# RWKV time mixing on one Trainium2 core: where a unit's columns lie in the mixed tiles of four batches

## The chip, the core and the metric

The kernel runs on one core of a Trainium2 chip. The metric is the device time of one execution in microseconds (us). The five engines of the core are written as in the profile: PE is TensorE (matmuls; PEld is its loading of weights), DVE is VectorE, ACT is ScalarE, POOL is GpSimd, SP is the queue that only starts transfers here. Each engine works through its own list of instructions in order, and the engines wait for each other by semaphores, which are counters that an instruction raises when it is done.

## The reference

Every token is mixed with the token before it, in two mixtures that matter here (the key projection never reaches the output):

```python
xv = x * time_mix_v + x_prev * (1 - time_mix_v)
xr = x * time_mix_r + x_prev * (1 - time_mix_r)
v = xv @ value_weight
r = xr @ receptance_weight
out = (sigmoid(r) * v) @ output_weight
```

x has 16 batches of 2048 tokens with 256 features. Features are the contraction of the first two products, so the tokens are transposed first: features on the 128 partitions, in two halves called `ko` 0 and 1, tokens along the columns.

## The kernel before

**Units and pairs.** The work is cut into 64 units of 512 tokens (`TU`), four to a batch; two units make a pair. Three tiles matter for each pair. `xt` holds the transposed tokens. `mix` holds the two mixtures m = 0 (receptance) and m = 1 (value) of a pair: 128 partitions, and per m and `ko` 1024 columns, so m takes 2048 elements of a partition's row, with `ko` 0 in the first 1024 of them and `ko` 1 in the second. `mix` rotates over three buffers. `z_sb` holds sigmoid(r) * v of one unit.

**A mixture is a product and a sum.** The token mix is folded into the weights: the tile needs only (previous token) * c plus (token). The product, one per pair, m and `ko`, covers 1024 columns and goes to DVE (`scale`, L353), ACT (`scale_act`, L631) or POOL (`scale_pool`, L363). The sum (`add`, L375) is one DVE instruction per unit and m, over both `ko`, 1024 elements, in place on `mix`.

**One unit on PE.** In program order, for unit g: four matmuls of 512 columns into `psum_r` (`project`, L383, m = 0; the order is output half, then `ko` 0, `ko` 1), eight matmuls of 256 columns into `psum_o` for unit g - 2 (`out_matmuls`, L412), four matmuls into `psum_v` (L383, m = 1). `psum_r`, `psum_v` and `psum_o` have one buffer each. ACT takes the sigmoid of `psum_r` (L651) and copies `psum_o` out (L464); DVE makes `z_sb` from the sigmoid and `psum_v` (L690).

**One unit on DVE.** From unit 10 on, the order in iteration g is: at even g the product of m = 0, `ko` 0 for the pair that begins with g + 2; then the sum of m = 1 for unit g + 1 (in the code `sums`); then `z_sb` of unit g; then the sum of m = 0 for unit g + 2 (in the code `held`). POOL makes one product in each iteration, after the sum of m = 1, and ACT one product at even g.

**The batches concerned.** Batches 10 to 13 (`STAGED_PAIRS`), units 40 to 55, eight pairs, get their transposed tokens by DMA from a copy in DRAM, as plain columns in the order of the tokens. Their stores want each partition to hold runs of tokens, so unit h of a pair takes columns q * 8 + h * 4 + i (q from 0 to 127, i from 0 to 3): runs of four columns, one run in two. `tokens` gives the view of `xt`, `mixed` the view of `mix`, and both use `unit_cols`. Products over a pair take all 1024 columns; sums and matmuls of one unit take its runs. Batches 14 and 15 and all earlier ones keep runs of 128 columns.

**Order.** The program order is written out by hand and not changed by a scheduler; the waits are derived from it by the framework, which looks at which columns of a tile each instruction reads and writes.

Of the kernel before, what the change touches and what calls it, by code (L numbers as in the profile page):

```python
# [15 lines left out]
def kernel(  # L16
# [31 lines left out]
    UJ = 4  # L48
    TU = UJ * P
# [63 lines left out]
    xt = {}  # L113
# [199 lines left out]
    def slots(piece, off=0):  # L313

        b, _, lo, hi = piece
        j = lo // P + (lo // TU if b < BYUNIT else 0) + off
        return slice(j, j + (hi - lo) // P)

    def unit_cols(cols, lo, hi):

        if hi - lo > TU:
            return cols
        assert hi - lo == TU
        return cols.rearrange("p k (q h i) -> p k q h i", h=2, i=UJ)[:, :, :, lo // TU % 2]

    def tokens(piece, off, ko=None):

        b, _, lo, hi = piece
        if b in STAGED_PAIRS:
            pair = lo // (2 * TU) * 2 * TU + off  # L330
            cols = unit_cols(xt[b][:, :, pair : pair + 2 * TU], lo, hi)
            return cols if ko is None else cols[:, ko]
        if b < STAGED:
            cols = xt[b][:, slots(piece, off)]
        else:
            cols = xt[b][:, :, off + lo : off + hi].rearrange("p k (j c) -> p j k c", c=P)
        return cols if ko is None else cols[:, :, ko]

    def mixed(piece, ko=None):
        b, m, lo, hi = piece  # L340
        cols = mix[(b * S + lo) // (2 * TU)][:, m]
        if b in STAGED_PAIRS:
            cols = cols.rearrange("p j k c -> p (j k c)").rearrange("p (k t) -> p k t", k=KO)
            cols = unit_cols(cols, lo, hi)
            return cols if ko is None else cols[:, ko]
        j = lo // P % (2 * UJ)
        cols = cols[:, j : j + (hi - lo) // P]
        return cols if ko is None else cols[:, :, ko]

    def scale(piece, kos=(0, 1)):  # L350
        b, m, _, _ = piece
        for ko in kos:
            nc.vector.tensor_scalar(  # L353
                out=mixed(piece, ko),
                in0=tokens(piece, 0, ko),
                scalar1=c_sb[:, m, ko : ko + 1],
                scalar2=None,
                op0=ALU.mult,
            )

    def scale_pool(piece, after):
        b, m, _, _ = piece
        op = nc.gpsimd.tensor_scalar(  # L363
            out=mixed(piece, 1),
            in0=tokens(piece, 0, 1),
            scalar1=c_sb[:, m, 1:2],
            scalar2=1.0,
            op0=ALU.mult,
            op1=ALU.mult,
        )  # L370
        tc.add_manual_dep(op.ins, after.ins.name, SYNC, reason="one at a time")

    def add(piece):
        b = piece[0]
        return nc.vector.tensor_tensor(  # L375
            out=mixed(piece), in0=mixed(piece), in1=tokens(piece, 1), op=ALU.add
        )
# [261 lines left out]
    for g in range(NU - 1):  # L639
# [61 lines left out]
        if g in STAGE_AT:  # L701
            b = STAGE_AT[g]
# [41 lines left out]
```

## Time and profile before

| what | value |
|---|---|
| median of three runs | 200.34 us (200.04 to 200.56) |
| the profiled execution | 200.75 us, span of its instructions 198.9 us |
| PE busy | 193.8 us, 97% |
| DVE busy | 183.8 us, 92% |
| ACT busy | 177.0 us, 89% |
| POOL busy | 86.8 us, 44% |
| sum, L375, on `xt_both` | 112 of 696 ns |
| product on DVE, L353, 1024 columns | 40 of 481 ns |
| product on POOL, L363, 1024 columns | 54 of 1121 ns |
| product on ACT, L631, 1024 columns | 14 of 1161 ns |

The span runs from the first instruction to the last; 1.85 us of the profiled time lie outside it. A matmul's record is longer than its turn: records of one group overlap, so the time from one group's start to the next is what the group costs on PE.

### The profile page before, as it was taken

What the parts mean: (1) busy time and instruction counts of PE and PEld (TensorE: products, weight loads), DVE (VectorE), ACT (ScalarE), POOL (GpSimd) and SP (SyncE); (2) the same over time, 40 slices, a digit from 0 to 9 for tenths busy, and PEclk for the clock granted to TensorE, in tenths of its full rate; (3) what the DMA queues carried; (4) which work ended last, traced back from release to release, by engine and by line L of the source; (5) the groups of instructions that cost most, each with busy time, mean ns of one, the idle gap of its engine ahead of it and who ended that gap; (6) DMA issues with size and microseconds to landing.
All of it is one profiled execution on the core that took longest, in us unless ns stands there. A gap on an engine that the chain in (4) does not pass through costs nothing.

```text
span 198.9 us, 3759 instructions
## 1 busy us (share of the span) xinstructions
PE 193.8 (97%) x1368; PEld 123.5 (62%) x1368; DVE 183.8 (92%) x287; ACT 177.0 (89%) x197; POOL 86.8 (44%) x117
## 2 busy tenths in 40 slices
PE   8999999999999999999999999999999999999992
PEld 4656676666666666666666566656655666666661
DVE  0899999999999999999999999999999999999972
ACT  3699899999999999999999999998888888899972
POOL 2846442443675634624424474444443344444200
PEclk9999999999999999999999999999999999999998
DMA  5999999999999999999999999999999999999585
GB/s 176 236 184 216 221 278 274 270 256 260 247 384 272 292 315 321 290 226 222 234 276 290 416 293 222 208 273 228 290 340 420 415 412 422 415 417 413 244 319 202
DMA packets 36553, 58.13 MB, mean 292 GB/s; under 512 B 26068, under 2 KB 27448, under 8 KB 32312
## 3 DMA queue, kind: packets, MB, share of 16 engines
q1 hardware_dynamic: 32368, 41.34, 59.7%
q0 software_dynamic: 4016, 16.44, 41.2%
q8 instruction: 10, 0.16, 0.3%
q10 hardware_dynamic: 152, 0.13, 0.2%
q14 instruction: 7, 0.06, 0.1%
HBM read 34.34 MB, written 39.90 MB: 373 GB/s over the span
## 4 chain that ended last, share of the span: by engine, by line
PE 87%; DVE 5%; DMA 3%; SPq 1%; issue 1%; POOL 1%; ACT 1%; DVEq 0%; POOLq 0%
PE psum_v L383 26%; PE psum_r L383 26%; PE psum_o L412 26%; PE ps_t L271 7%; DMA w_f<-in_value_weight_dram 3%; DVE z_sb L690 2%; DVE mix L375 1%; DVE mix L353 1%; SPq L173 1%; PE ps_t L412 1%; ACT s_sb L651 1%; PE ps_t L383 0%; POOL x_bf L161 0%; POOL mix L363 0%; DVE w_bf L587 0%
## 5 line engine op out<-in xcount | busy, mean ns | idle before, releaser
L363 POOL TENSOR_SCALAR mix<-xt_both,c_sb 128x1024 bf16<-128x1024 bf16 (+1 forms) x55 | 61.2, 1113 | 86.8 <-DVE mix L375 74.4
L690 DVE TENSOR_TENSOR z_sb<-s_sb,psum_v 128x1024 bf16<-128x1024 bf16 (+1 forms) x64 | 76.7, 1199 | 3.4 <-PE psum_v L383 2.5
L375 DVE TENSOR_TENSOR mix<-mix,xt_both 128x1024 bf16<-128x1024 bf16 x112 | 76.8, 696 | 1.4
L383 PEld LDWEIGHTS <-w_bf 128*128 128x128 bf16 x516 | 48.7, 97 | 40.2 <-DVE mix L375 0.8
L651 ACT ACTIVATE s_sb<-psum_r 128x1024 bf16<-128x1024 f32 x63 | 65.2, 1035 | 7.5 <-PE psum_r L383 7.2
L383 PE MATMUL psum_v<-mix,w_bf 128*128 128x512 bf16 (+1 forms) x256 | 65.9, 379 | 0.1
L383 PE MATMUL psum_r<-mix,w_bf 128*128 128x512 bf16 (+1 forms) x252 | 64.8, 379 | 0.2 <-DVE mix L375 0.2
L412 PE MATMUL psum_o<-wo_bf,z_sb 128*128 128x256 bf16 x486 | 63.3, 272 | 0.2 <-DVE z_sb L690 0.2
L412 PEld LDWEIGHTS <-z_sb 128*128 128x128 bf16 x512 | 51.7, 103 | 18.6 <-DVE z_sb L503 0.7
L464 ACT COPY o_sb<-psum_o 128x1024 f32<-128x1024 f32 x50 | 51.2, 1024 | 5.1 <-PE psum_o L412 5.1
L288 ACT COPY xt_both<-ps_t 128x1024 bf16<-128x1024 bf16 x32 | 32.8, 1036 | 0.0
L271 PEld LDWEIGHTS <-x_bf 128*128 128x128 bf16 x304 | 19.8, 98 | 8.6 <-DMA x_bf<-in_x_dram 0.7
L271 PE MATMUL ps_t<-ident,x_bf 128*128 128x128 bf16 x304 | 22.7, 219 | 0.3 <-DMA x_bf<-in_x_dram 0.3
L353 DVE TENSOR_SCALAR mix<-xt_both,c_sb 128x1024 bf16<-128x1024 bf16 (+1 forms) x47 | 21.2, 460 | 0.0
L631 ACT ACTIVATE mix<-xt_both,c_sb 128x1024 bf16<-128x1024 bf16 x14 | 16.2, 1161 | 0.0
L375 DVE TENSOR_TENSOR mix<-mix,xt_first 128x1024 bf16<-128x1024 bf16 x15 | 10.6, 714 | 0.1
L464 ACT COPY x_bf<-psum_o 128x1024 f32<-128x1024 f32 x10 | 10.2, 1015 | 0.0
L353 DVE TENSOR_SCALAR mix<-xt_first,c_sb 128x512 bf16<-128x512 bf16 x22 | 6.6, 353 | 0.2
L288 ACT COPY xt_first<-ps_t 128x1024 bf16<-128x1024 bf16 x6 | 6.1, 1024 | 0.0
L161 POOL DMA_DIRECT2D x_bf<-in_x_dram x8 | 5.2, 656 | 0.0
L550 POOL COPY xt_first<-xt_first 128x254 bf16<-128x254 bf16 x5 | 2.0, 395 | 6.8 <-DVE mix L375 6.8
L363 POOL TENSOR_SCALAR mix<-xt_first,c_sb 128x512 bf16<-128x512 bf16 x6 | 4.1, 689 | 1.5 <-DVE mix L375 1.0
(70 smaller groups left out, 54.7 us busy)
## 6 DMA issues: line engine op xcount, KB each, us to landing
out_dram<-o_sb SPq DMA_DIRECT2D x24, 1024.0 KB, 12.8
x_bf<-in_x_dram POOLq DMA_DIRECT2D x8, 1024.0 KB, 16.5
x_natural<-in_x_dram POOLq DMA_DIRECT2D x4, 1024.0 KB, 13.7
out_dram<-x_bf SPq DMA_DIRECT2D x4, 1024.0 KB, 14.5
x_natural<-in_x_dram POOLq DMA_DIRECT2D x4, 512.0 KB, 14.0
x_bf<-in_x_dram POOLq DMA_DIRECT2D x6, 256.0 KB, 6.6
out_dram<-x_bf SPq DMA_DIRECT2D x6, 256.0 KB, 2.2
o_sb<-in_x_dram SPq DMA_DIRECT2D x4, 256.0 KB, 4.1
```

Of the source, the lines that this page charges most:

```text
L161: return nc.gpsimd.dma_start(out=x_bf[b], in_=rows(b), max_dma_last_dim=run)
L271: nc.tensor.transpose(out=ps[:, jj], in_=src[:, jj, ko * P : (ko + 1) * P], identity=idn)
L288: nc.scalar.copy(out=xt[b][:, j0 : j0 + UJ], in_=ps)
L353: nc.vector.tensor_scalar(out=mixed(piece, ko), in0=tokens(piece, 0, ko), scalar1=c_sb[:, m, ko : ko + 1], scalar2=None, op0=ALU.mult,)
L363: op = nc.gpsimd.tensor_scalar(out=mixed(piece, 1), in0=tokens(piece, 0, 1), scalar1=c_sb[:, m, 1:2], scalar2=1.0, op0=ALU.mult, op1=ALU.mult,
L375: return nc.vector.tensor_tensor(out=mixed(piece), in0=mixed(piece), in1=tokens(piece, 1), op=ALU.add)
L383: nc.tensor.matmul(out=ps[:, mo, :], lhsT=w_bf[:, m, ko, mo * P : (mo + 1) * P], rhs=mixed((b, m, e * TU + lo, e * TU + hi), ko), start=(k ...
L412: nc.tensor.matmul(out=ps[:, j, :], lhsT=slot[:, ko, j], rhs=wo_bf[:, ko, :], start=(ko == 0), stop=(ko == KO - 1),)
L464: nc.scalar.copy(out=o[:, j0 : j0 + UJ, :], in_=ps)
L631: nc.scalar.activation(out=mixed(piece, ko), in_=tokens(piece, 0, ko), func=ACT.Copy, scale=c_sb[:, m, ko : ko + 1],)
L651: nc.scalar.activation(out=s_sb, in_=ps_r, func=ACT.Sigmoid)
L690: nc.vector.tensor_tensor(out=z_sb[:, :, c : c + n], in0=s_sb[:, :, c : c + n], in1=ps_v[:, :, c : c + n], op=ALU.mult,)
```

## The change

In batches 10 to 13 the two units of a pair no longer alternate in `mix` every four columns; unit 0 has columns 0 to 511 and unit 1 columns 512 to 1023. `xt` stays in token order. So a product, which covers the pair, now reads 1024 columns in one run and writes runs of four, by turns into the first and the second half; a sum reads `xt` in runs of four as before, but reads and writes `mix` in one run of 512 per `ko`; a matmul reads one run of 512. The number of instructions and their order on every engine stay as they are.

```diff
-    def unit_cols(cols, lo, hi):
+    def unit_cols(cols, order, lo, hi):
+        cols = cols.rearrange(f"p k ({order}) -> p k q h i", h=2, i=UJ)
         if hi - lo > TU:
             return cols
         assert hi - lo == TU
-        return cols.rearrange("p k (q h i) -> p k q h i", h=2, i=UJ)[:, :, :, lo // TU % 2]
+        return cols[:, :, :, lo // TU % 2]
...
-            cols = unit_cols(xt[b][:, :, pair : pair + 2 * TU], lo, hi)
+            cols = unit_cols(xt[b][:, :, pair : pair + 2 * TU], "q h i", lo, hi)
...
             cols = cols.rearrange("p j k c -> p (j k c)").rearrange("p (k t) -> p k t", k=KO)
-            cols = unit_cols(cols, lo, hi)
+            cols = unit_cols(cols, "h q i", lo, hi)
```

## The prediction

> **What bounds the kernel now.** I read the page first, then the chain of work that ended last in order of time, then the timeline of one pair. The page:
>
> ```profile
> PE 193.8 (97%) x1368; PEld 123.5 (62%) x1368; DVE 183.8 (92%) x287; ACT 177.0 (89%) x197; POOL 86.8 (44%) x117
> ...
> PE 87%; DVE 5%; DMA 3%; SPq 1%; issue 1%; POOL 1%; ACT 1%; DVEq 0%; POOLq 0%
> ```
>
> PE is busy 97% and is 87% of the chain. In the stage concerned the chain is PE alone; from it, the groups around its entry and two after its end:
>
> ```profile
> 128.29 0.86 PE psum_v L383 x4
> 129.15 0.90 PE psum_r L383 x4
> 130.05 0.87 PE psum_o L412 x8
> 130.93 0.90 PE psum_v L383 x4
> 131.83 0.90 PE psum_r L383 x4
> ...
> 172.84 0.87 PE psum_o L412 x8
> 173.71 0.86 PE psum_v L383 x4
> 174.58 0.86 PE psum_r L383 x4
> ```
>
> Units 40 to 55 begin with psum_r at 129.15. There a group of four matmuls takes 0.90 us instead of 0.86: the alternating runs of four cost PE 0.036 us a group (0.900 - 0.864). A pair takes 5.35 us here (131.83 to 137.18) and 5.20 after the stage (174.58 to 179.78). The pair around unit 46, timeline of all engines:
>
> ```profile
> 144.14 1.06 PE L383 MATMUL psum_v<-mix,w_bf 128*128 128x512 bf16 x4
> ...
> 145.05 1.06 PE L383 MATMUL psum_r<-mix,w_bf 128*128 128x512 bf16 x4
> ...
> 145.31 1.22 DVE L690 TENSOR_TENSOR z_sb<-s_sb,psum_v 128x1024 bf16<-128x1024 bf16 x1 [0.18 <-PE psum_v L383]
> ...
> 146.45 0.69 DVE L375 TENSOR_TENSOR mix<-mix,xt_both 128x1024 bf16<-128x1024 bf16 x1
> 146.53 2.13 SPq L433 DMA_DIRECT2D out_dram<-o_sb  x3
> 146.71 1.56 PEld L383 LDWEIGHTS <-w_bf 128*128 128x128 bf16 x8
> 146.82 1.06 PE L383 MATMUL psum_v<-mix,w_bf 128*128 128x512 bf16 x4
> 147.06 0.48 DVE L353 TENSOR_SCALAR mix<-xt_both,c_sb 128x1024 bf16<-128x1024 bf16 x1
> ...
> 147.45 0.69 DVE L375 TENSOR_TENSOR mix<-mix,xt_both 128x1024 bf16<-128x1024 bf16 x1
> ```
>
> psum_v of unit 45 starts at 144.14, psum_r of unit 46 follows at 145.05 without a gap. The z of unit 45 can start only when that psum_v is done (145.31); behind it on DVE comes the sum of m = 0 for unit 47 (146.45 to 147.14), then the product and the sum of m = 1 for unit 47 (147.45 to 148.14). PE needs none of these two sums before unit 47, one unit later: that distance hides DVE.
>
> [...] sums with runs of four at 146.45 take 0.69 us, as the mean of all sums, 696 ns. [...] Beside z[...] POOL runs here without stretching it (1.22 us).
>
> **The change, part by part.** *Matmuls.* 16 units x 2 groups x 0.036 us = 1.15 us less on PE.
>
> *Waits.* The compiled programs have the same instructions in the same order on all engines, and the same waits on DVE, ACT, POOL and SP. On PE they differ, in each of the eight pairs. For units 40 and 41 (counts of DVE's semaphore; 199 and 200 are unit 40's sums of m = 0 and 1, 201 is z of unit 39, 202 and 204 are unit 41's sums, 203 a product):
>
> ```
> instruction on PE                   waits for DVE, before    after
> psum_r of 40, weights of matmul 1   199                      199
> psum_r of 40, weights of matmul 2   -                        202
> psum_v of 40, matmul 1              201                      - (covered by 202)
> psum_v of 40, weights of matmul 2   -                        204
> psum_r of 41, weights of matmul 1   202                      - (covered by 202)
> ```
>
> The second matmul of an even unit reads `ko` 1 of its own half, columns 1024 to 1535. The other unit's sum writes 512 to 1023 and 1536 to 2047; the columns in between are not touched, but first to last they enclose 1024 to 1535. I infer that the framework compares these extents; the waits themselves are in the program. With alternating runs it kept the units apart. So PE waits for a sum that it doesn't need, one unit too early.
>
> *The price of the wait for 202.* Let T be the start of the last matmul of psum_v of the odd unit before: 144.14 + 3 x 0.227 = 144.82. z starts at T + 0.49, the sum of m = 0 ends at 147.14 = T + 2.32. From a DVE end to the PE start it releases is 0.05 us (the chain has issue for 0.05 us between z at 191.70 and psum_o at 191.75). So matmul 2 starts at T + 2.37. Without a wait and with contiguous reads it starts two turns after T, at T + 0.43. **The stall is 1.94 us a pair.** No cover is left: z itself needs psum_v, the last PE work before the stall, and the psum_o of the unit stands behind the waiting matmul.
>
> *The new period.* From matmul 2 to the next T: three turns (0.65), psum_o (0.87), psum_v (0.86), psum_r (0.86), psum_o (0.87), three turns (0.65) = 4.76. Period 2.37 + 4.76 = 7.13 against 5.35: +1.78. Eight pairs: **+14.2 us**; the same from the stalls less the gain, 8 x 1.94 - 1.15 = 14.4. I take 14.3.
>
> *The wait for 204.* The second sum ends 148.14 = T + 3.32, released T + 3.37. psum_v's matmul 2 is due at T + 2.37 + 0.65 + 0.87 + 0.22 = T + 4.11. It costs nothing, with 0.74 us to spare.
>
> *What is late next.* z of the even unit starts at T + 5.0 and ends at 6.25; psum_v of the odd unit needs it at T + 6.5: free. ACT: sigmoid at T + 3.2, copy of psum_o at 4.1, product at 5.0, sigmoid of the odd unit 6.1 to 7.1, needed by z at T + 7.6: 0.5 us to spare. Stores start later, none sooner. Nothing queued is recovered later, since PE is the chain on both sides of the stage.
>
> *Products.* Eight on DVE, eight on ACT, sixteen on POOL now write runs of four by turns to two halves. No row shows this write. DVE: at best 0.48 us as now; at worst [...] z's 1.22 us; the added 0.74 us fall before the sum counted 204, whose spare is 0.74 us: 0. (Without the stall this would set the pace: DVE needs 5.18 us of a 5.35 us pair, its idle time being 0.17.) ACT: up to 0.5 us more is free. POOL: as now 1.12 us, since 8 rows of 128 cost it what one run does[...]. POOL's product at the odd unit starts with z (145.31 both) and now ends as z does[...]. [...] I take no change on all three. Sums: -0.02 to +0.02 us each, taken as 0; the one behind z counts, 8 x 0.02 = 0.2 us.
>
> **Sum.** Span 198.9 + 14.3 = 213.2, profiled time 200.75 + 14.3 = 215.05; the profile lay 0.41 above the median, so the median becomes **214.6 us**.
>
> **The rivals.** *POOL is slower too:* 214.6 + 4 = 218.6. For: such a write is not in the trace. [...] *The clock drops:* PE is idle 1.94 of 7.13 us[...]. [...] *Not slower, the waits are met when PE arrives:* then only the gain of 1.15 us is left, 199.2. It takes the sum counted 202 being ready within 0.43 + 1.15 / 8 = 0.57 us after T, while z alone ends at T + 1.71; for it speaks only that the chain now shows PE without gaps. *No change in effect:* the gain of 1.15 exactly eaten by DVE at 5.35 us a pair, 200.3; it needs the same absence of stalls.
>
> **How the numbers follow.** The computed case 0.75 (range 213.4 to 215.8: 0.15 us per stall either way, eight times), POOL slower 0.16, clock 0.05, waits without effect 0.03, no change 0.01. The range of 8 in 10 or more is 213.0 to 218.8: the computed case and the slower POOL. By the bound of 0.3%, about 0.6 us, which is what this kernel's runs can tell: faster 0.03, same 0.01, slower 0.96.
>
> **What would show it.** PE's share falls to about 90% ((193.8 - 1.15) / 213.2). About 15 us of idle time appear before the weight loads of psum_r and psum_v, released by DVE's sums, eight times, 1.9 us each. The chain shows in each pair: psum_v, z, sum, psum_r. Groups of four matmuls take 0.86 us in the stage. DVE and ACT wait for PE in it. A product on POOL over 1.2 us, or a clock under 0.95 in the stage, would put the time above the range; PE gapless in the stage would make the prediction wrong altogether.

## The result, and the profile after

The changed kernel takes 215.19 us (median of four runs, 214.74 to 215.29) against 200.22 us before (four runs; the table above has three of them): ratio 1.0741, 95% interval 1.0719 to 1.0762. It is slower by about 15 us; 214.6 us was forecast. The profiled execution has a span of 213.0 us, 14.1 more than before.

The page of the changed kernel, busy shares and the chain by engine; then its row of slices for PE:

```profile
PE 193.5 (91%) x1368; PEld 122.7 (58%) x1368; DVE 184.4 (87%) x287; ACT 176.7 (83%) x197; POOL 86.6 (41%) x117
...
PE   8999999999999999999999996697669766999993
...
PE 79%; DVE 12%; DMA 2%; issue 2%; SPq 1%; ACT 1%; POOL 1%; DVEq 0%; ACTq 0%; POOLq 0%
```

PE does the same work (193.5 us against 193.8), but it is no longer the chain alone: DVE's share rose from 5% to 12%, and the slices with 6 and 7 tenths lie in the stage of units 40 to 55. The chain that ended last, in order of time, through one pair of that stage (start us, us, what):

```profile
149.38 0.88 PE psum_v L384 x4
...
150.35 1.22 DVE z_sb L691
151.57 0.61 DVE mix L376
152.18 0.05 issue
152.23 0.82 PE psum_r L384 x3
153.05 0.87 PE psum_o L413 x8
153.92 0.86 PE psum_v L384 x4
154.79 0.86 PE psum_r L384 x4
155.65 0.87 PE psum_o L413 x8
...
159.37 0.82 PE psum_r L384 x3
```

Where psum_r followed psum_v without a gap, there now stand z (1.22 us), the sum behind it and the way back to PE, and psum_r is on the chain with three matmuls instead of four: its first has run before the stall. From 152.23 to the same place in the next pair, 159.37, it is 7.14 us, where the kernel before took 5.35. The groups of four take 0.86 us, where they took 0.90 in this stage before: the gain in reading is there. The same pair on the timeline:

```profile
149.22 1.03 PE L384 MATMUL psum_v<-mix,w_bf 128*128 128x512 bf16 x4
...
150.08 0.38 PE L384 MATMUL psum_r<-mix,w_bf 128*128 128x512 bf16 x1
...
150.35 1.22 DVE L691 TENSOR_TENSOR z_sb<-s_sb,psum_v 128x1024 bf16<-128x1024 bf16 x1 [0.17 <-PE psum_v L384]
...
151.49 0.68 DVE L376 TENSOR_TENSOR mix<-mix,xt_both 128x1024 bf16<-128x1024 bf16 x1
...
152.22 0.33 PEld L384 LDWEIGHTS <-w_bf 128*128 128x128 bf16 x3 [2.26 <-DVE mix L376]
152.23 0.82 PE L384 MATMUL psum_r<-mix,w_bf 128*128 128x512 bf16 x3 [1.77 <-DVE mix L376]
...
152.89 1.04 PE L413 MATMUL psum_o<-wo_bf,z_sb 128*128 128x256 bf16 x8
```

One matmul of psum_r starts at 150.08, and the next, due one turn of 0.216 us later, at 152.23: a stall of 1.93 us. The two bracketed numbers are the same stall seen by two rows. The weight load of the first matmul ended at 149.96, 0.12 us before that matmul started, so the idle time of the loads is longer (2.26); that matmul's record lasts 0.38 us and not its turn of 0.216, so the idle time of the matmuls is shorter (1.77). The price of a stall on PE is read from start to start. It is the same in all eight pairs: the page has 14.2 us of this idle time in the matmul row, 8 x 1.77. And the psum_o that stands behind the waiting matmul waited too: it starts at 152.89, although the z that it reads was done at 148.97 and its buffer was copied out at 150.73. The prediction had counted on this; PE without gaps in the kernel before could not show it.

The products, which now write in two halves, kept their times. The stage's rows, medians of the times in ns (minimum/median/maximum), for DVE and POOL in the changed kernel:

```profile
L354 DVE TENSOR_SCALAR mix<-xt_both,c_sb x8: 480/490/495, 130.7 to 180.7; 128x1024 bf16<-128x1024 bf16 x8
```

```profile
L364 POOL TENSOR_SCALAR mix<-xt_both,c_sb x16: 1118/1118/1119, 129.1 to 181.8; 128x1024 bf16<-128x1024 bf16 x16
```

In the same stage before, the medians were 481 and 1122 ns; ACT's product has 1162 ns in both, and the sum 684 ns against 685. So neither products nor sums got slower by more than 9 ns an instruction.

### The profile page after: what moved, and what is told of

The parts are those of the page before. It is cut to its first block, busy times and chain, and to the rows that moved or that the text cites. A ratio compares the mean times of both kernels' runs of the same rounds, so it can differ in the third digit from the quotient of the medians.

```text
span 213.0 us, 3759 instructions
## 1 busy us (share of the span) xinstructions
PE 193.5 (91%) x1368; PEld 122.7 (58%) x1368; DVE 184.4 (87%) x287; ACT 176.7 (83%) x197; POOL 86.6 (41%) x117
## 4 chain that ended last, share of the span: by engine, by line
PE 79%; DVE 12%; DMA 2%; issue 2%; SPq 1%; ACT 1%; POOL 1%; DVEq 0%; ACTq 0%; POOLq 0%
PE psum_v L384 24%; PE psum_r L384 23%; PE psum_o L413 23%; PE ps_t L271 7%; DVE z_sb L691 7%; DVE mix L376 4%; DMA w_f<-in_value_weight_dram 2%; DVE mix L354 1%; SPq L173 1%; PE ps_t L413 1%; ACT s_sb L652 1%; ACT x_bf L465 0%; PE ps_t L384 0%; POOL x_bf L161 0%; POOL mix L364 0%
## 5 line engine op out<-in xcount | busy, mean ns | idle before, releaser
L384 PEld LDWEIGHTS <-w_bf 128*128 128x128 bf16 x516 | 48.2, 98 | 55.6 <-DVE mix L376 19.2
L384 PE MATMUL psum_r<-mix,w_bf 128*128 128x512 bf16 (+1 forms) x252 | 65.6, 378 | 14.2 <-DVE mix L376 14.2
L465 ACT COPY o_sb<-psum_o 128x1024 f32<-128x1024 f32 x50 | 51.2, 1024 | 5.1 <-PE psum_o L413 5.0
L632 ACT ACTIVATE mix<-xt_both,c_sb 128x1024 bf16<-128x1024 bf16 x14 | 16.3, 1162 | 0.0
```

Of the source, the lines that this page charges most:

```text
L384: nc.tensor.matmul(out=ps[:, mo, :], lhsT=w_bf[:, m, ko, mo * P : (mo + 1) * P], rhs=mixed((b, m, e * TU + lo, e * TU + hi), ko), start=(k ...
L465: nc.scalar.copy(out=o[:, j0 : j0 + UJ, :], in_=ps)
L632: nc.scalar.activation(out=mixed(piece, ko), in_=tokens(piece, 0, ko), func=ACT.Copy, scale=c_sb[:, m, ko : ko + 1],)
```

## Experiments

The theory: PE waits for sums that it doesn't need, and the place of those sums on DVE sets the price. The rival: the new column order is slow in itself, by its writes to two halves or otherwise. The kernel before, run beside these experiments, had a median of 200.68 us; the expectations start from 200.2, so about 0.5 us by which a measured time exceeds them is no miss.

**The waits alone.** The column order of the kernel before, with the two waits of the changed kernel put in by hand:

```diff
+                if b in STAGED_PAIRS and e % 2 == 0 and (mo, ko) == (0, 1):
+                    other = sum_of[b, m, (e + 1) * TU, (e + 2) * TU]
+                    tc.add_manual_dep(op.ins, other.ins.name, SYNC, reason="the other unit's sum")
```

> The kernel before with its old column order; on PE the second matmul of psum_r and of psum_v of each even unit is made to wait for the sum of the odd unit, as in the changed kernel. If the waits are the cause: the stalls of 1.94 us in eight pairs with the 1.15 us of slower matmul reads still there, a period of 7.13 + 0.15 = 7.28 us, 200.2 + 8 x 1.93 = 215.7 us (215.0 to 216.5). If the new column order itself is slow (writes in two halves, reads of 512): 200.2 us, since nothing of it is here, apart from what the waits cost beside.

Measured: 216.28 us (216.17 to 216.52), ratio 1.0782 (1.0763 to 1.0800). Its chain through a pair:

```profile
138.37 0.85 PE psum_r L387 x3
139.22 0.87 PE psum_o L419 x8
140.09 0.90 PE psum_v L387 x4
140.99 0.90 PE psum_r L387 x4
...
142.77 0.92 PE psum_v L387 x4
...
143.78 1.22 DVE z_sb L697
145.00 0.61 DVE mix L377
...
145.66 0.85 PE psum_r L387 x3
```

The ring is the one of the changed kernel, with groups of 0.90 us: 145.66 - 138.37 = 7.29 us, expected 7.28. The waits suffice for the whole loss, with no column moved, and the slower reads come on top of it (7.29 us a pair against 7.14).

**The products alone.** Products write in the new order; sums and matmuls keep the old columns. The sums then add products of other tokens:

```diff
-            cols = unit_cols(cols, "h q i", lo, hi)
+            cols = unit_cols(cols, "h q i" if hi - lo > TU else "q h i", lo, hi)
```

> The changed kernel in which only the products write in the new order; sums and matmuls use the old columns, so the output is not the reference's: the sums add the products of other tokens. Its waits are those of the kernel before. If the waits are the cause: 200.2 us within 0.3%, products 0.48 us on DVE and 1.12 us on POOL. If the writes in runs of four to two halves are slow anywhere: above 201 us, up to 215.

Measured: 200.63 us, ratio 1.0005 (0.9985 to 1.0025); product medians 490 ns on DVE, 1124 on POOL, 1166 on ACT. The writes in two halves cost nothing that shows, although DVE has only 0.17 us of a pair to spare here. With the experiment before, the rival is out as far as the writes go; sums and matmuls in the new order are tested by the last two experiments.

**One mixture at a time.** New order for m = 0 alone, then for m = 1 alone; each keeps one of the two waits:

```diff
-            cols = unit_cols(cols, "h q i", lo, hi)
+            cols = unit_cols(cols, "h q i" if m == 0 else "q h i", lo, hi)
```

> New column order for m = 0 (receptance) alone: of the two new waits only the one for the sum behind z is left, at psum_r. If each wait costs what its place says: stall 1.94 us a pair, psum_v still read in runs of four: period 2.37 + 0.65 + 0.87 + 0.90 + 0.86 + 0.87 + 0.68 = 7.20 us, 200.2 + 8 x 1.85 = 215.0 us (214.4 to 215.8). If the cost lay in the number of waits or of rearranged tiles: about half of 15, 207.7 us.

Measured: 215.70 us (215.65 to 215.93), ratio 1.0754 (1.0736 to 1.0772). From one resumption of psum_r to the next on its chain: 7.22 us, expected 7.20. The first wait carries the loss alone.

> New column order for m = 1 (value) alone: only the wait of psum_v for the odd unit's sum of m = 1 is left, which is covered in the changed kernel. Without the first stall it is uncovered: the sum ends 3.32 us after the last matmul of the psum_v before, PE goes on at T + 3.37 instead of T + 2.20; then 0.65 + 0.90 + 0.87 + 0.65, period 6.44 us against 5.35, 200.2 + 8 x 1.09 = 208.9 us (208.3 to 209.8). If the wait were free as in the changed kernel: 199.6 us, half of the gain in matmul reads. If the cost goes by rearranged tiles: 207.7 us.

Measured: 209.73 us (209.14 to 210.59), ratio 1.0463 (1.0425 to 1.0501). Its chain through a pair:

```profile
138.44 0.82 PE psum_v L384 x3
139.26 0.90 PE psum_r L384 x4
140.16 0.87 PE psum_o L413 x8
141.03 0.88 PE psum_v L384 x4
...
142.00 1.22 DVE z_sb L691
143.22 0.60 DVE mix L376
143.83 0.40 DVE mix L354
144.23 0.61 DVE mix L376
...
144.88 0.39 PE psum_v L384
```

144.88 - 138.44 = 6.44 us, as expected (the chain lists the group that begins at 144.88 in pieces). This wait cost nothing in the changed kernel, because the other stall had already held PE for longer; with that one gone it costs 9 us. Two waits don't add up: 15.0 and 9.1 us alone, 15 together.

**The sum ahead of z.** As the kernel with m = 0 alone, but on DVE the sum that PE waits for stands ahead of z at odd units:

```diff
+        for p in [q for q in held[g] if g % 2 and q[0] in STAGED_PAIRS]:
+            held[g].remove(p)
+            last = add(p)
         ps_v = ps_v_pool.tile([P, KO, TU], FP32, name="psum_v")
         project(ps_v, g, 1)
```

> As the one with the new order for m = 0 alone, the wait for the sum is kept, but on DVE that sum stands ahead of z of the unit before instead of behind it. If the price is the place of the sum behind z: PE no longer waits 1.94 us for it; z of the odd unit comes up to 0.4 us later, and by DVE's order z to z takes 3.0 and 2.4 us, a period of 5.3 to 5.4 us, 200.7 us (199.6 to 201.5). If any such wait costs a stall whatever stands before it: as without the move, 215.0 us.

Measured: 204.42 us (204.06 to 204.62), ratio 1.0183 (1.0170 to 1.0196). 11.3 of the 15.0 us are back, so the place behind z was most of the price, but the expected 200.7 us was missed. Its timeline:

```profile
138.05 1.22 DVE L694 TENSOR_TENSOR z_sb<-s_sb,psum_v 128x1024 bf16<-128x1024 bf16 x1 [0.57 <-PE psum_v L384]
...
139.19 1.89 DVE L376 TENSOR_TENSOR mix<-mix,xt_both 128x1024 bf16<-128x1024 bf16 x3
...
140.41 0.38 PE L384 MATMUL psum_r<-mix,w_bf 128*128 128x512 bf16 x1
...
141.13 0.33 PEld L384 LDWEIGHTS <-w_bf 128*128 128x128 bf16 x3 [0.84 <-DVE mix L376]
...
143.83 1.22 DVE L694 TENSOR_TENSOR z_sb<-s_sb,psum_v 128x1024 bf16<-128x1024 bf16 x1 [0.56 <-PE psum_v L384]
```

The sum is now the third in a row of three behind the z of the even unit, and ends at 141.08. PE goes on at 141.13 instead of 140.63, 0.5 us late. The stall is shorter, but a ring through both engines remains: z and the three sums 3.08 us (138.05 to 141.13), three turns of psum_r, psum_o, psum_v and the start of the next z at 143.83, together 5.78 us a pair; 8 x (5.78 - 5.35) = 3.4 us, where 3.7 were measured. DVE is not the limit, for it stands idle for 0.56 us before that z. The edit also makes POOL's product of an odd unit wait for the moved sum, since it waits for the last sum made (`last`); with DVE idle before z, nothing shows that this costs time. I had put z and sums against DVE's own order only and had left the way back through PE out.

**Odd sums in two halves.** The changed kernel, with the sum of an odd unit as two instructions, one per `ko`:

```diff
+        if b in STAGED_PAIRS and piece[2] // TU % 2:
+            for ko in range(KO):
+                op = nc.vector.tensor_tensor(
+                    out=mixed(piece, ko), in0=mixed(piece, ko), in1=tokens(piece, 1, ko), op=ALU.add
+                )
+            return op
```

> The changed kernel with each sum of an odd unit cut into its two ko halves, two instructions of 512 elements instead of one of 1024: the waits of even units for odd sums are gone, and DVE has four instructions for two in each pair. If the waits are the loss: the stalls go; DVE then sets the pace with 5.18 + 2 x (0.07 to 0.10) = 5.32 to 5.38 us a pair, 200.0 to 200.5 us. If the layout is slow in itself: it stays near 215 us.

Measured: 200.55 us, ratio 0.9997 (0.9987 to 1.0008); the expected range ended at 200.5. The whole loss is gone with every column where the changed kernel has it. The timeline:

```profile
140.84 0.81 DVE L378 TENSOR_TENSOR mix<-mix,xt_both 128x512 bf16<-128x512 bf16 x2
...
141.97 0.75 DVE L378 TENSOR_TENSOR mix<-mix,xt_both 128x512 bf16<-128x512 bf16 x2
...
142.64 1.21 DVE L697 TENSOR_TENSOR z_sb<-s_sb,psum_v 128x1024 bf16<-128x1024 bf16 x1
...
142.89 1.04 PE L419 MATMUL psum_o<-wo_bf,z_sb 128*128 128x256 bf16 x8
...
143.90 1.02 PE L390 MATMUL psum_v<-mix,w_bf 128*128 128x512 bf16 x4
...
144.76 1.03 PE L390 MATMUL psum_r<-mix,w_bf 128*128 128x512 bf16 x4
```

The psum_r of the even unit (144.76) again follows psum_v after one turn of the group. The two halves of a sum together take 0.81 us (m = 0) and 0.75 us (m = 1), where the whole sum took 0.69 in the kernel before: 0.18 us more a pair, within the 2 x (0.07 to 0.10) that had been estimated. What the reads gain goes to DVE, which has no gap in the pair: the z of the even unit ends at 143.85, and the psum_v of the odd unit, which needs the buffer that this z reads, starts at 143.90, 1.01 us after psum_o instead of 0.87. From z to z of the pair it is 139.70 to 145.03, 5.33 us, a little under the 5.35 of the kernel before.

**Each unit's columns in one piece.** The two `ko` of a unit side by side, then the other unit:

```diff
-            cols = cols.rearrange("p j k c -> p (j k c)").rearrange("p (k t) -> p k t", k=KO)
-            cols = unit_cols(cols, "h q i", lo, hi)
+            cols = cols.rearrange("p j k c -> p (j k c)")
+            cols = cols.rearrange("p (h k q i) -> p k q h i", h=2, k=KO, i=UJ)
+            if hi - lo == TU:
+                cols = cols[:, :, :, lo // TU % 2]
```

> Contiguous reads without the new waits: in batches 10 to 13 a mixed tile holds unit 0's 512 columns of ko 0 and of ko 1 and then unit 1's, so no unit's columns lie between the first and last column of the other's; the waits in the program are those of the kernel before. If the waits alone are the loss: PE reads in 0.86 us a group, period 5.20 us, 200.2 - 8 x 0.144 = 199.1 us (198.8 to 199.5); DVE needs 5.18 us of it, and its products at 490 ns instead of 481 leave it at 5.19. If DVE or POOL becomes the bound with the new writes: no gain, 200.2 us or more. If contiguous columns are slow in themselves: near 215 us.

Measured: 199.74 us (199.17 to 200.20) against 200.68, ratio 0.9950 (0.9935 to 0.9966). Its chain:

```profile
141.09 0.86 PE psum_v L386 x4
141.95 0.86 PE psum_r L386 x4
142.81 0.87 PE psum_o L415 x8
143.69 0.86 PE psum_v L386 x4
144.55 0.86 PE psum_r L386 x4
145.41 0.87 PE psum_o L415 x8
146.29 0.65 PE psum_v L386 x3
```

PE is gapless again with groups of 0.86 us, its share of the chain 90%, and a pair takes 146.29 - 141.09 = 5.20 us, as expected (of the last group the trace has three records). The gain is 0.9 us or 0.5% of 200.68, where 8 x 0.144 = 1.15 us was worked out; the median lies 0.2 us above the range that was expected from 200.2. This version beats both kernels, the one before by 0.5%: contiguous reads are worth what the profile before said, and the changed kernel lost only by the waits that came with its order.

## Why the prediction was right

**The bound and the gain.** The reading gain, 0.900 to 0.864 us a group, is in the chain of the changed kernel and, in the last experiment, in the time (0.9 of 1.15 us).

**The stall.** Forecast 1.94 us a pair, measured 1.93. Forecast period 7.13 us, measured 7.14. Span forecast 213.2 us, measured 213.0. So the forecast came true by its mechanism and not by luck. The median, 215.19, is 0.6 us above the 214.6 for another reason: the profiled run of the kernel before lay 0.41 us above its median, that of the changed kernel, 214.74, is the fastest of four. The terms hold one by one: with T = 149.22 + 0.65 = 149.87, z starts at T + 0.48 (0.49), the sum ends at 152.17, T + 2.30 (2.32), and matmul 2 starts at T + 2.36 (2.37).

**The second wait.** It was costed at nothing with 0.74 us of cover; psum_v stays whole in the chain of the changed kernel, and the kernel with m = 1 alone shows the price without the cover. The text had said that about 15 us of idle time would stand before the weight loads of psum_r and psum_v. It stands before psum_r alone, as the text's own sum implies, and its weight-load row has 2.26 us each time, not 1.9.

**What is late next.** ACT's order came as worked out: its sigmoid of the even unit at 153.09 is T + 3.22 (forecast 3.2), the copy at 154.01 T + 4.14 (4.1), the product at 154.90 T + 5.03 (5.0). None of them holds PE.

**The products.** Left unchanged in the sum: +9 ns on DVE, -4 ns on POOL. The rival with a slower POOL falls with this row; the 4 us at which it was put were an estimate of mine that no trace showed. PE's granted clock was 1.00 from 129 to 186 us, through 1.93 us of idling in each 7.14 us, and 1.000 over the run, where the kernel before had 0.997. That settles the clock rival, which had no trace behind it either.

**The cause of the waits.** The prediction inferred that the framework compares the first and last columns of what two instructions touch. That fits the changed kernel, and the two versions that run without the stall: sums cut per `ko`, and each unit in one piece. It does not fit the kernel before: there, too, the sum of unit 1 reaches from column 4 to 2047 and encloses, first to last, all that unit 0 reads of `ko` 1 (1024 to 2043), and no wait was made. So the rule is another one, or has more to it; it stays open. The number did not hang on it, since the waits themselves were taken from the program. What is shown is that the time follows the waits: put in by hand they bring the whole loss, and the two versions of the new order whose traces show no such stall lose nothing.

## What to carry to other kernels

A layout also decides what a framework takes for a dependence. Here one sum that wrote two runs of 512 columns, with a run between them that PE reads early, brought a wait that nothing needed; cut into one instruction per run, or with each unit in one piece, the stall was gone. So compare the wait lists of the two programs before costing any instruction. Here the wait was priced by what stood in front of the awaited sum on its own engine: it cost 15.0 us with the sum behind the 1.22 us z and 3.7 with the sum ahead of it, and the 15.0 are more than ten times the gain that came with it. A wait that costs nothing behind a stall may cost much once the stall is mended: the one for the sum of m = 1 cost 9.1 us alone.

## What the runs showed of the hardware

Three things had not been shown by the profile before. Products that wrote runs of four bf16, by turns to two places 1 KB apart, took nearly the time of contiguous ones: on DVE 490 against 481 ns, on POOL 1118 against 1122, on ACT 1162 in both. Behind a waiting matmul the next ones waited too, although what they read was there: psum_o started at 152.89, with its z done at 148.97 and its buffer copied out at 150.73. And PE's granted clock was 1.00 from 129 to 186 us, with a gap of 1.93 us in every 7.14.
